# Attention scores: the second product of each head on half the rows, heads issued in pairs

## The chip, the cores and the metric

The kernel runs on one core of one Trainium2 chip. The metric is the device time of one execution in microseconds (us); where several runs are compared, their median. One core has TensorE (PE, matrix products; the loading of its stationary operand is listed apart as PEld), VectorE (DVE), ScalarE (ACT), GpSimd (POOL) and the queue that issues transfers (SP).

## What is computed

A two-layer trunk: in each layer a feed-forward sublayer, a mixer and a second feed-forward sublayer, for 512 latent tokens and 128 context tokens (640 columns, five tiles of 128). Both mixers hold an attention of 8 query heads of width 64 on 2 key heads; beside it runs a recurrent branch. The change touches the attention scores alone. The reference has

```
s = jnp.einsum('bqhgd,bkhd->bhgqk', q, k).astype(F32) * (q.shape[-1] ** -0.5)
if mask is not None: s = jnp.where(mask, s, NEG_INF)
...
p = jax.nn.softmax(s, axis=-1)
return jnp.einsum('bhgqk,bkhd->bqhgd', p.astype(v.dtype), v)
```

In the first mixer a latent tile sees its neighbour tiles (a band of +-128) and the 128 context keys, with a sink; in the second it sees all 512 latent keys and the 128 context keys. The context tile sees itself.

## The kernel before

Every product works on numbers split into a high part (rounded to the matmul format) and a low part (the remainder). Most products are three matmuls (`mm3`, high-high, high-low, low-high). The scores have a cheaper form, since a head has only 64 rows and TensorE takes 128: `q_stack` puts the high half of a head's query on 64 rows of a tile and its low half on the other 64. For heads 0 and 2 of a group of four the high half lies on rows 0 to 63, for heads 1 and 3 on rows 64 to 127. `att_keys` writes the keys' high part on both halves of the rows of `kk[:, 0]`, and their low part on both halves of `kk[:, 1]`. In `att_probs` the helper `scores` (L684) then needs two matmuls of 128 rows for a run of key tiles: stacked query times high keys, plus stacked query times low keys, added up in one PSUM bank.

`attention` goes through 10 steps: two key heads g, for each the five query tiles j. For a step `att_probs` takes the four heads in turn: it asks for a bank (`bank`, L112: PSUM tags a2 and b, two buffers each, used by other stages too), issues the scores, adds the mask on DVE, takes the row maximum on DVE, and has ACT compute the exponentials into SBUF. After heads 1 and 3 it yields. Then `att_out` transposes the probabilities on PE (tile pT, tag b), splits them on ACT and DVE and multiplies by the values (pv). In the first mixer a tile sees three or four key tiles, in one or two runs of neighbouring tiles; heads 0 to 2 have one bank each (a2 or b), head 3 one of three tiles and one of a single tile. In the second mixer a tile sees five key tiles, and every head has two parts, three tiles (384 columns, tag a2) and two tiles (256 columns, tag b). The fifth query tile has one key tile; all four heads then share one bank.

`weave` runs the attention's generator side by side with those of the projections (tiles pj and pn), one step of each in turn, so that one step of a projection (24 matmuls) follows each pair of heads in the text. The order on each engine is laid down before the run by the framework's planner, which starts from the order of the text and takes a later instruction where an earlier one isn't ready by its own reckoning (its operands, or a free bank). Each engine then works through its list in that order.

`mm` (L136) issues every matmul, so all of them have that line: they are told apart by tiles. The score matmuls are `s<-att`.

Of the kernel before, what the change touches and what calls it, by code (L numbers as in the profile page):

```python
# [17 lines left out]
P = 128  # L18
# [31 lines left out]
class Net:  # L50
# [628 lines left out]
    def att_probs(self, q, ks, tiles, masks, nsink, room, out):  # L679


        nc = self.nc
        mx, nm, su = self.sm(8, "mx"), self.sm(4, "nm"), self.sm(12, "su")

        def scores(o, hd, t0, t1):
            for n, k in enumerate(ks):
                self.mm(o, q[:, hd], k[:, t0 * P:t1 * P], n == 0, n == 1)

        def minus(c):
            if nsink is None:  # L690
                self.ts(nm[:, c], mx[:, c], -1.0, ALU.mult)
            else:
                self.stt(nm[:, c], mx[:, c], -1.0, nsink[:, c], ALU.mult, ALU.min)

        two = []
        if len(tiles) == 1:
            p = self.bank("a2", "s1")
            for hd in range(4):
                scores(p[:, hd * P:(hd + 1) * P], hd, tiles[0], tiles[0] + 1)
            nc.vector.tensor_reduce(out=mx[:, 0:4], in_=p.rearrange("p (a b) -> p a b", a=4), op=ALU.max, axis=AX.X)  # L700
            minus(slice(0, 4))
            for hd in range(4):
                r = room[hd][0][:, 0:P]
                self.act(r, p[:, hd * P:(hd + 1) * P], AF.Exp, bias=nm[:, hd:hd + 1], accum_out=su[:, hd:hd + 1])
                out.append([r])
            yield
        else:
            for hd in range(4):
                pos, parts, at = 0, [], []
                for r in room[hd]:  # L710
                    ts = tiles[pos:pos + r.shape[-1] // P]
                    pos += len(ts)
                    if not ts:
                        break
                    n = len(parts)
                    p = self.bank(("a2", "b")[n if len(room[hd]) > 1 else hd % 2], "s1")
                    o = 0
                    while o < len(ts):
                        e = o + 1
                        while e < len(ts) and ts[e] == ts[e - 1] + 1:  # L720
                            e += 1
                        scores(p[:, o * P:e * P], hd, ts[o], ts[e - 1] + 1)
                        o = e
                    p = p[:, :len(ts) * P]
                    if masks and n == 0:
                        v = p.rearrange("p (a b) -> p a b", b=P)[:, masks[0]]
                        self.tt(v, v, masks[1], ALU.add)
                    nc.vector.tensor_reduce(out=mx[:, 4 * n + hd:4 * n + hd + 1], in_=p, op=ALU.max, axis=AX.X)
                    parts.append((p, r[:, :len(ts) * P]))
                    at += [r[:, i * P:(i + 1) * P] for i in range(len(ts))]  # L730
                c = slice(hd, hd + 1)
                if len(parts) > 1:
                    self.tt(mx[:, c], mx[:, c], mx[:, 4 + hd:5 + hd], ALU.max)
                minus(c)
                for n, (p, r) in enumerate(parts):
                    self.act(r, p, AF.Exp, bias=nm[:, c], accum_out=su[:, 4 * n + hd:4 * n + hd + 1])
                if len(parts) > 1:
                    two.append(hd)
                out.append(at)
                if hd % 2 == 1:  # L740
                    yield
        if two:
            a, b = two[0], two[-1] + 1
            self.tt(su[:, a:b], su[:, a:b], su[:, 4 + a:4 + b], ALU.add)
        if nsink is not None:
            self.tt(su[:, 8:12], nm, nsink, ALU.subtract)
            self.act(su[:, 8:12], su[:, 8:12], AF.Exp)
            self.tt(su[:, 0:4], su[:, 0:4], su[:, 8:12], ALU.add)
        nc.vector.reciprocal(out=su[:, 4:8], in_=su[:, 0:4])
        for hd in range(4):  # L750
            n = len(tiles)
            for r in room[hd]:
                w = min(n, r.shape[-1] // P)
                n -= w
                if w:
                    self.ts(r[:, :w * P], r[:, :w * P], su[:, 4 + hd:5 + hd], ALU.mult)
# [810 lines left out]
```

## Time and profile before

| | |
|---|---|
| median of 3 runs | 2791.62 us (2791.42 to 2794.95) |
| profiled execution, whole | 2794.22 us |
| its span | 2792.4 us |
| PE busy | 2691.6 us, 96% |
| PEld busy | 2583.1 us, 93% |
| DVE, ACT, POOL busy | 1781.6, 947.6, 250.5 us |
| score matmuls | 260, in two stretches: 595 to 760 us and 1900 to 2110 us |

The profiled execution lies 2.6 us above the median, inside what the three runs show; 1.8 us of it lie outside the span. Matmul durations overlap, since a matmul's recorded end is modelled: what one matmul costs is read from the distance between the starts of matmuls that follow each other, not from its duration.

### The profile page before, as it was taken

What the parts mean: (1) busy time and instruction counts of PE and PEld (TensorE: products, weight loads), DVE (VectorE), ACT (ScalarE), POOL (GpSimd) and SP (SyncE); (2) the same over time, 40 slices, a digit from 0 to 9 for tenths busy, and PEclk for the clock granted to TensorE, in tenths of its full rate; (3) what the DMA queues carried; (4) which work ended last, traced back from release to release, by engine and by line L of the source; (5) the groups of instructions that cost most, each with busy time, mean ns of one, the idle gap of its engine ahead of it and who ended that gap; (6) DMA issues with size and microseconds to landing.
All of it is one profiled execution on the core that took longest, in us unless ns stands there. A gap on an engine that the chain in (4) does not pass through costs nothing.

```text
span 2792.4 us, 46713 instructions
## 1 busy us (share of the span) xinstructions
PE 2691.6 (96%) x19121; PEld 2583.1 (93%) x19121; DVE 1781.6 (64%) x3498; ACT 947.6 (34%) x1946; POOL 250.5 (9%) x293
## 2 busy tenths in 40 slices
PE   7999999999999999999999999999999899999998
PEld 4999999898888999999999999987888789999997
DVE  4967864676767976533896773375677688333335
ACT  3321221455554421311522122154555444112112
POOL 1000000410013000000400000051100031000003
PEclk9999999999999999999999999998999999999999
DMA  7553543221122544422264452121011225213210
GB/s 244 174 151 115 166 121 85 71 73 48 39 74 79 171 133 124 133 64 68 69 186 125 123 170 77 53 85 50 24 46 59 70 78 145 74 54 99 69 46 38
DMA packets 307186, 270.52 MB, mean 97 GB/s; under 512 B 13834, under 2 KB 257308, under 8 KB 306972
## 3 DMA queue, kind: packets, MB, share of 16 engines
q1 hardware_dynamic: 306612, 267.39, 32.2%
q8 instruction: 150, 2.46, 0.4%
q14 instruction: 64, 0.52, 0.1%
q10 hardware_dynamic: 360, 0.14, 0.0%
HBM read 258.31 MB, written 9.18 MB: 96 GB/s over the span
## 4 chain that ended last, share of the span: by engine, by line
PE 77%; DVE 11%; DMA 4%; ACT 4%; issue 2%; POOL 1%; DVEq 0%; ACTq 0%; SPq 0%; POOLq 0%
PE ps L136 36%; PE po L136 23%; PE pj L136 6%; PE pn L136 3%; DMA rawa<-in_ada_w 2%; DVE acc L133 2%; DVE w L126 2%; PE pv L136 1%; DMA raw<-in_ffn_w 1%; PE pT L139 1%; PE s L136 1%; DVE x L126 1%; DVE h L126 1%; DVE x L133 1%; DVE sum L126 1%
## 5 line engine op out<-in xcount | busy, mean ns | idle before, releaser
L136 PE MATMUL ps<-h,w 128*128 128x256 f32 (+1 forms) x7584 | 1123.5, 309 | 6.0 <-DVE h L126 3.2
L136 PEld LDWEIGHTS ps<-h,w 128*128 128x128 f32 x7584 | 1116.3, 190 | 8.6 <-DVE h L126 4.2
L136 PE MATMUL po<-g,wv 128*128 128x256 f32 (+1 forms) x4224 | 634.1, 310 | 8.2 <-DVE x L133 5.4
L136 PEld LDWEIGHTS po<-g,wv 128*128 128x128 f32 x4224 | 623.0, 189 | 15.7 <-DVE x L133 6.2
L133 DVE SCALAR_TENSOR_TENSOR x<-po,mod,x 128x128 f32<-128x128 f32 (+1 forms) x576 | 235.8, 435 | 280.5 <-PE po L136 278.2
L126 DVE TENSOR_TENSOR w<-raw,w 128x1024 fp32r<-128x1024 f32 x208 | 254.4, 1228 | 124.4 <-ACT w L123 123.6
L133 DVE SCALAR_TENSOR_TENSOR acc<-rawa,sc,acc 128x512 f32<-128x512 f32 x448 | 319.6, 757 | 11.7 <-DMA rawa<-in_ada_w 11.6
L123 ACT ACTIVATE wv<-raw 128x1024 fp32r<-128x1024 f32 x120 | 124.4, 1056 | 578.0 <-PE po L136 456.7
L123 ACT ACTIVATE w<-raw 128x1024 fp32r<-128x1024 f32 x208 | 218.6, 1056 | 160.5 <-issue 81.3
L485 POOL TENSOR_TENSOR ssq<-ssq,sq 128x384 f32<-128x384 f32 (+1 forms) x84 | 84.8, 1010 | 1726.4 <-ACT sq L123 1725.8
L123 ACT ACTIVATE g<-gt 128x384 fp32r<-128x384 f32 (+1 forms) x176 | 82.1, 466 | 403.8 <-DVE gt L126 403.7
L126 DVE TENSOR_TENSOR wv<-raw,wv 128x1024 fp32r<-128x1024 f32 x120 | 147.0, 1230 | 104.6 <-ACT wv L123 104.5
L126 DVE TENSOR_TENSOR gt<-sl,ps 128x384 f32<-128x384 f32 (+1 forms) x176 | 85.2, 484 | 181.5 <-PE ps L136 176.9
L136 PE MATMUL pj<-h,w 128*128 128x384 f32 (+1 forms) x864 | 150.6, 317 | 0.6 <-ACT mi L123 0.6
L123 ACT ACTIVATE sl<-ps 128x384 f32<-128x384 f32 (+1 forms) x176 | 76.0, 433 | 200.2 <-PE ps L136 199.9
L136 PE MATMUL ps<-h,wv 128*128 128x256 f32 (+1 forms) x864 | 139.4, 312 | 3.1 <-ACT h L123 1.3
L136 PE MATMUL pn<-w,h 128*128 128x256 f32 x960 | 139.5, 288 | 1.3 <-ACT mi L123 0.9
L136 PEld LDWEIGHTS pj<-h,w 128*128 128x128 f32 x864 | 132.5, 193 | 3.5 <-issue 1.2
L136 PEld LDWEIGHTS ps<-h,wv 128*128 128x128 f32 x864 | 128.4, 189 | 6.3 <-DVE h L126 3.0
L136 PEld LDWEIGHTS pn<-w,h 128*128 128x128 f32 x960 | 124.2, 190 | 4.2 <-ACT mi L123 1.1
L136 PE MATMUL pj<-h,wv 128*128 128x256 f32 (+1 forms) x672 | 114.1, 317 | 3.9 <-DVE t L126 1.8
L136 PEld LDWEIGHTS pj<-h,wv 128*128 128x128 f32 x672 | 100.7, 192 | 7.3 <-issue 2.1
(327 smaller groups left out, 2516.8 us busy)
## 6 DMA issues: line engine op xcount, KB each, us to landing
raw<-in_ffn_w SPq DMA_DIRECT2D x264, 512.0 KB
rawa<-in_ada_w SPq DMA_DIRECT2D x144, 512.0 KB
raw<-in_w_in_odd SPq DMA_DIRECT2D x18, 512.0 KB
raw<-in_w_in_even SPq DMA_DIRECT2D x14, 512.0 KB
raw<-in_w_in_even SPq DMA_DIRECT2D x16, 256.0 KB
raw<-in_w_out_even SPq DMA_DIRECT2D x8, 512.0 KB
raw<-in_w_in_odd SPq DMA_DIRECT2D x16, 256.0 KB
raw<-in_w_out_odd SPq DMA_DIRECT2D x8, 512.0 KB
```

Of the source, the lines that this page charges most:

```text
L123: return self.nc.scalar.activation(out=out, in_=in_, func=func, **k)
L126: return self.nc.vector.tensor_tensor(out=out, in0=in0, in1=in1, op=op)
L133: return self.nc.vector.scalar_tensor_tensor(out=out, in0=in0, scalar=s, in1=in1, op0=op0, op1=op1)
L136: return self.nc.tensor.matmul(out=out, lhsT=lhsT, rhs=rhs, start=start, stop=stop)
L139: self.nc.tensor.transpose(out, in_, self.ident[:in_.shape[0], :in_.shape[0]])
L485: nc.gpsimd.tensor_tensor(out=sums[1], in0=sums[1], in1=sq, op=ALU.add)
```

## The change

For a run of key tiles the first product stays as it is. The second product is issued apart (`rest`) and takes only the 64 rows on which the head's high query half lies: high query times low keys. The product of the two low halves is left out. The weights and the moving operand of this matmul are cut to rows 0 to 63 for heads 0 and 2, and to rows 64 to 127 for heads 1 and 3. The heads of a pair (0 and 1, 2 and 3) get their banks together, and their matmuls are issued for each run as: first product of one, first product of the other, second product of one, second product of the other. Masks, maxima and exponentials follow after both heads' scores. The step with one key tile keeps its two products on 128 rows.

```
         def scores(o, hd, t0, t1):
-            for n, k in enumerate(ks):
-                self.mm(o, q[:, hd], k[:, t0 * P:t1 * P], n == 0, n == 1)
+            self.mm(o, q[:, hd], ks[0][:, t0 * P:t1 * P], True, False)
+
+        def rest(o, hd, t0, t1):
+            r = slice(64 * (hd % 2), 64 * (hd % 2) + 64)
+            self.mm(o, q[r, hd], ks[1][r, t0 * P:t1 * P], False, True)
...
         if len(tiles) == 1:
             p = self.bank("a2", "s1")
             for hd in range(4):
-                scores(p[:, hd * P:(hd + 1) * P], hd, tiles[0], tiles[0] + 1)
+                c = slice(hd * P, (hd + 1) * P)
+                scores(p[:, c], hd, tiles[0], tiles[0] + 1)
+                self.mm(p[:, c], q[:, hd], ks[1][:, tiles[0] * P:tiles[0] * P + P], False, True)
...
+            banks = {}
             for hd in range(4):
+                if hd % 2 == 0:
+                    lists = []
+                    for h2 in (hd, hd + 1):
+                        pos, lst = 0, []
+                        for n, r in enumerate(room[h2]):
+                            ts = tiles[pos:pos + r.shape[-1] // P]
+                            pos += len(ts)
+                            if not ts:
+                                break
+                            p = banks[h2, n] = self.bank(("a2", "b")[n if len(room[h2]) > 1 else h2 % 2], "s1")
+                            o = 0
+                            while o < len(ts):
+                                e = o + 1
+                                while e < len(ts) and ts[e] == ts[e - 1] + 1:
+                                    e += 1
+                                lst.append((p[:, o * P:e * P], h2, ts[o], ts[e - 1] + 1))
+                                o = e
+                        lists.append(lst)
+                    for n in range(max(map(len, lists))):
+                        for f in (scores, rest):
+                            for lst in lists:
+                                if n < len(lst):
+                                    f(*lst[n])
...
-                    p = self.bank(("a2", "b")[n if len(room[hd]) > 1 else hd % 2], "s1")
-                    o = 0
-                    while o < len(ts):
-                        e = o + 1
-                        while e < len(ts) and ts[e] == ts[e - 1] + 1:
-                            e += 1
-                        scores(p[:, o * P:e * P], hd, ts[o], ts[e - 1] + 1)
-                        o = e
-                    p = p[:, :len(ts) * P]
+                    p = banks[hd, n][:, :len(ts) * P]
```

## Rows read from the trace of the kernel before

**Rows 1.** The page: busy time by engine, and the chain that ended last.

```profile
PE 2691.6 (96%) x19121; PEld 2583.1 (93%) x19121; DVE 1781.6 (64%) x3498; ACT 947.6 (34%) x1946; POOL 250.5 (9%) x293
...
PE 77%; DVE 11%; DMA 4%; ACT 4%; issue 2%; POOL 1%; DVEq 0%; ACTq 0%; SPq 0%; POOLq 0%
```

**Rows 2.** Busy time in the two stretches: us, each engine's (instructions), clock, DMA.

```profile
595.00:760.00 165.00, 159.72 (x1079) 145.64 (x1079) 116.79 (x310) 91.64 (x240) 9.64 (x17) 0.99 0.17 47
1900.00:2110.00 210.00, 198.50 (x1377) 172.87 (x1376) 146.70 (x386) 118.52 (x315) 16.81 (x18) 0.96 0.13 37
```

**Rows 3.** Tile s by form: weight rows*columns, moving rows x columns, count | busy, mean.

```profile
L136 PE MATMUL s<-att 128*128 128x384 f32 x100 | 29.2, 374 | 4.6 <-ACT pq L123 4.0 <-ACT E L123 0.4
L136 PE MATMUL s<-att 128*128 128x256 f32 x80 | 17.5, 303 | 0.1
L136 PE MATMUL s<-att 128*128 128x128 f32 x68 | 10.5, 257 | 0.0
...
L136 PE MATMUL s<-att 128*128 128x512 f32 x12 | 4.2, 402 | 0.3 <-ACT bm L123 0.3
```

**Rows 4.** Timeline of PE, first mixer: start us, us, engine, line, tiles, form, count.

```profile
598.18 3.04 PE L136 MATMUL pn<-w,h 128*128 128x256 f32 x24
601.06 1.03 PE L136 MATMUL s<-att 128*128 128x256 f32 x8
601.92 3.09 PE L136 MATMUL pn<-w,h 128*128 128x256 f32 x24
...
606.21 4.43 PE L136 MATMUL pj<-h,w 128*128 128x384 f32 x24
610.48 0.38 PE L139 MATMUL pT<-ident,E 128*128 128x128 f32 x2
610.70 0.27 PE L139 MATMUL pT<-ident,bm 128*128 128x128 f32 x1
```

**Rows 5.** Timeline of PE around matmuls with 64 weight rows (nmu, ab).

```profile
751.16 1.21 PE L136 MATMUL pj<-h,w 128*128 128x256 f32 x8
752.30 0.79 PE L136 MATMUL ab<-ma,identr 64*128 64x384 f32 x4
...
754.55 0.85 PE L136 MATMUL pn<-w,h 128*128 128x256 f32 x5
755.33 0.50 PE L136 MATMUL nmu<-ma,identr 64*128 64x256 f32 x2
755.76 1.22 PE L136 MATMUL pn<-w,h 128*128 128x256 f32 x8
756.91 0.50 PE L136 MATMUL nmu<-ma,identr 64*128 64x256 f32 x2
```

**Rows 6.** Timeline of PE: a matmul with 64 weight columns among full ones.

```profile
632.32 0.40 PE L136 MATMUL pv<-pr,vals 128*64 128x512 f32 x1
632.55 0.62 PE L136 MATMUL s<-att 128*128 128x512 f32 x2
633.02 0.63 PE L136 MATMUL pv<-pr,vals 128*64 128x512 f32 x2
```

**Rows 7.** Timeline of PE: matmuls on 32 weight columns each, at the kernel's start.

```profile
16.51 0.62 PE L136 MATMUL ada<-rawa,scz 128*32 128x512 f32 x2 [0.23 <-DMA rawa<-in_ada_w]
```

**Rows 8.** Groups by form, 16.4 to 17.7 us: count | busy us, mean ns | idle.

```profile
L136 PE MATMUL ada<-rawa,scz 128*32 128x512 f32 x4 | 1.1, 604 | 0.2 <-DMA rawa<-in_ada_w 0.2
```

**Rows 9.** Timeline of PE, first mixer: two heads of one step.

```profile
623.80 0.62 PE L136 MATMUL s<-att 128*128 128x512 f32 x2
...
628.15 0.40 PE L136 MATMUL s<-att 128*128 128x512 f32 x1
```

**Rows 10.** Timeline of PE, second mixer: scores among a projection's matmuls.

```profile
2044.35 0.60 PE L136 MATMUL s<-att 128*128 128x384 f32 x2
...
2045.32 0.51 PE L136 MATMUL s<-att 128*128 128x256 f32 x2
...
2047.28 0.61 PE L136 MATMUL s<-att 128*128 128x384 f32 x2
```

## The prediction

> **What bounds the kernel now.** I read the page first. TensorE is busy for 2691.6 of 2792.4 us, 96%, and the chain that ended last runs on it for 77% of the span; VectorE has 64%, ScalarE 34% [rows 1]. So a change of the attention is worth what it does to PE's own list of matmuls, as long as nothing else becomes late. The score matmuls lie in two stretches, and the table of busy time by stretch shows there what the page shows for the whole: PE busy for 159.7 of 165 us and 198.5 of 210, at a granted clock of 0.99 and 0.96, with VectorE and ScalarE at 56 to 71% [rows 2]. PE is idle for 5.3 and 11.5 us, 16.8 together. That is all the slack that the two stretches have, and it belongs to PE's waits for the softmax, not to the matmuls.
>
> Next I counted the score matmuls by form: 100 of 384 columns, 80 of 256, 68 of 128 and 12 of 512, 260 in all, every one with 128 weight rows [rows 3]. 32 of the 128-column ones belong to the step with one key tile, which stays as it is. Of the other 228 half are second products: 50 of 384 columns, 40 of 256, 18 of 128, 6 of 512, that is 114 `rest` matmuls. They are 0.6% of PE's 19121 matmuls, so the whole change is about tens of us at the most.
>
> Then the price of one. A matmul's recorded duration overlaps its neighbours', so the reader should look at starts. 24 matmuls of 256 columns take from 598.18 to 601.06 us, 0.120 us each; 24 of 384 columns from 606.21 to 610.48, 0.178 each; two of 128 columns 0.11 each [rows 4]. Two of 512 take from 632.55 to 633.02, 0.235 each [rows 6]. These distances follow the columns, so no weight load lies open between them.
>
> **What the change can save.** The number of matmuls and weight loads stays. A matmul with 64 rows streams as many columns as one with 128, so alone it saves nothing. What can be saved is the second product of a pair's second head, if it runs beside the first head's on the other half of the rows. The loops give 56 pairs of `rest` and two without a partner (the lone tile of head 3 at j = 2, once for each g): 24 pairs of 384 columns, 20 of 256, 8 of 128, 2 of 512, and 2 of 512 with 384. At the prices above: 24 x 0.178 + 20 x 0.120 + 8 x 0.11 + 2 x 0.235 + 2 x 0.178 = 8.4 us, if every pair overlaps in full. No row of before has two matmuls on different halves of the rows back to back. The nearest are matmuls on different strips of 32 columns: two of 512 columns start and end within 0.62 us, hardly more than one of them lasts (mean 0.604), so strips of columns do run side by side [rows 7, 8]. I take full overlap for adjacent partners; the bounds are nothing and 8.4 us.
>
> **What a change of rows costs.** The kernel already has matmuls of the very form that `rest` gets, 64 weight rows by 128 columns: nmu (rows 0 to 63) and ab (rows 64 to 127) of the recurrent branch. They are the rows that decide the case [rows 5]. Between two groups of them eight full matmuls of 256 columns take from 751.16 to 752.30, 1.14 us, where 8 x 0.120 = 0.96 was due; five take 0.78 for 0.60; eight take 1.15 for 0.96. And two nmu of 256 columns take from 755.33 to 755.76, 0.43 for 0.24. So every stretch between two changes of form carries 0.18 to 0.19 us that its matmuls don't explain, on both sides. One excursion to 64 rows and back costs 0.37 us, whether it holds two matmuls or four. By these rows PE doesn't stream across the change: the pipeline has to run empty, and then the weight load of the next matmul lies open. A cut of the columns has no such price: a matmul of 64 weight columns is followed by a full one after 0.23 us, the ordinary distance of 512 columns [rows 6].
>
> The Trainium skill has a rule that speaks against the change: TensorEngine Tiling (Array Packing), Key Properties, says that a change of the tiling mode, not merely of the tile, drains TensorE. The rows with 64 weight rows agree; those with 64 weight columns don't show it, so the rule taken alone would price the pv matmuls too, and the measurement decides. With the rule and without a figure for it the sum could not be made; with the rows it can.
>
> **The sum.** If all partners stay adjacent, there are 58 excursions: 58 x 0.37 = 21.5 us, less the 8.4 saved, is +13.1 us. That is the lower bound of PE's own time. If every `rest` stands alone, 114 x 0.37 = 42.2 us and nothing saved: the upper one.
>
> Which is it? PE's list is laid out beforehand, and an instruction that isn't ready gives way to the next that is. The scores of a head are ready when its PSUM bank is free. In the text `rest` of the first head now stands behind the first product of the second, but if the second head's bank isn't free at that moment, `rest` of the first is ready and goes alone. In the first mixer at j = 0 the eight score matmuls of a pair stand together [rows 4]; there the partners will stay adjacent (4 pairs for each g), and I expect the same for the second pair at j = 1 (2 more). At j = 2 the two heads' scores lie 4.35 us apart, since the second waits for a bank of tag b, which the transposes use too [rows 9]; I count j = 2, j = 3 and the first pair of j = 1 as broken: 6 of 12 pairs for each g. That makes 12 adjacent pairs, 24 lone halves and 2 single ones, 38 excursions. In the second mixer the scores stand one by one among projection matmuls, about 1 to 3 us apart, as banks come free [rows 10], so I count all 32 pairs as broken, 64 excursions. Sum: 102 x 0.37 = 37.7 us, less what the 12 adjacent pairs save (2 x (2 x (0.120 + 0.11) + 0.178 + 0.11) = 1.5 us), is +36.2 us of PE time.
>
> Not all of it reaches the end. Of PE's 16.8 us of idle time [rows 2] a part is waiting for the softmax of an earlier head; matmuls that take longer in between use it up. A delay ahead of the scores pushes the softmax back as well and uses up nothing. Bounds 0 and 16.8 us; I take half, 8.4 us, leaving +27.8 us.
>
> Edits that I cost at nothing: the instructions on VectorE and ScalarE are the same in number and form. Their start moves: the first head's maximum now waits for the second head's first product and for the excursion, some 0.18 + 0.37 us. VectorE has 30% of the stretch free to cover that; if it hadn't, 16 pairs of heads in each stretch would add 32 x 0.55 = 18 us, which is within the upper half of the range together with the cushion. The new wait is that of a second head's first product for its bank; on PE the first head's `rest` and the projection's matmuls queue behind it where the planner's reckoning was too early, and VectorE's maximum waits with them. Before, PE lost 4.6 us in front of 384-column scores in that way, 4.0 of them for ScalarE [rows 3]; doubled, that is 5 us more, and with good timing nothing or a little less. I take zero and keep 5 for the range.
>
> From the profiled execution (2794.2 us) the sum gives 2822 us; it lies 2.6 above the median, so against the runs' median of 2791.6 I predict 2819.4 us.
>
> **The rivals.** (1) The planner keeps the partners adjacent nearly everywhere. Then +13.1, less a share of the cushion of about 4: 2801 us. For it speaks the order of the text, and [rows 4]; against it [rows 9, 10]. (2) The change pays: the 64-row matmuls of two heads run side by side and the change of form costs nothing, as with 64 columns [rows 6]. Then -8.4: 2783 us, faster. The point from which this decides is the price of an excursion: below 8.4 / 58 = 0.145 us the change gains. Against it stand all four stretches of [rows 5], at 0.37. By the Trainium skill (TensorE: Matmul & The Clock Gate, Part 3, The mechanism) matmuls on different row groups start about 4 ns apart; by that alone this rival would be the result, and no row of before shows it for rows. (3) The excursions happen, but PE's idle time swallows them: with adjacent partners the 13.1 us would fit into the 16.8 idle, and the time would stay within 0.2%, at about 2793. It needs the waits to lie behind the excursions everywhere. (4) Everything is broken up, nothing is absorbed, and the new bank waits add 5: up to 42.2 + 2 or 3 on the median, 2836 us. The edit that changes nothing, because `rest` would still be taken as a 128-row matmul, I exclude: nmu and ab are cut by the same slices of rows and stand as 64*128 in the trace.
>
> **How the numbers follow.** Forecast 0.60; rival 1 0.19; rival 2 0.06; rival 3 0.05; rival 4 0.10. About 0.2%, 5.6 us, is what a measurement of this kernel can tell from no change. Faster 0.06 (rival 2), same 0.06 (rival 3 and a little of rival 1), slower 0.88. The range leaves out rivals 2 and 3 and the far end of rival 4: 2800 to 2836 us. Everything in it is slower than before.
>
> **What would show it.** In the profile after, tile s should have 146 matmuls of form 128*128 and 114 of 64*128; wherever a 64*128 group begins or ends, the starts should lie some 0.18 us further apart than columns explain, and PE's idle time of kind "issue" should grow in both stretches. PE's count stays at 19121. Lone groups should outnumber pairs, above all in the second mixer. Outside the two stretches nothing should move. I am wrong if adjacent partners cost more than 0.37 us together (no overlap), if lone excursions are rare, or if the two stretches don't lengthen although the excursions are there.

## The result and the profile after

The changed kernel takes 2823.22 us (median of 5 runs, 2816.15 to 2823.36) against 2791.62 of before; the ratio is 1.0099 with an interval of 1.0088 to 1.0109, so it is slower by 25 to 30 us. The two medians lie 31.6 us apart, a little more than this interval, since the five runs spread over 7 us. The profiled execution took 2823.36 us with a span of 2821.6, 29.2 us more than before. Forecast were 2819.4 and a range of 2800 to 2836.

The page of the changed kernel, busy times and chain, answers to [rows 1]:

```profile
PE 2728.3 (97%) x19121; PEld 2591.9 (92%) x19121; DVE 1784.8 (63%) x3498; ACT 947.5 (34%) x1946; POOL 252.0 (9%) x293
...
PE 81%; DVE 9%; DMA 4%; ACT 2%; issue 2%; POOL 1%; SPq 0%; ACTq 0%; DVEq 0%; POOLq 0%
```

The counts are those of before on every engine. PE's busy time has grown by 36.7 us and that of its weight loads by 8.8, no other by more than 3.2, and the chain runs on PE for 81% of the span instead of 77%. The score matmuls of the changed kernel by form answer to [rows 3]:

```profile
L136 PE MATMUL s<-att 64*128 64x384 f32 x50 | 21.9, 448 | 0.0
L136 PE MATMUL s<-att 128*128 128x384 f32 x50 | 18.7, 378 | 2.1 <-ACT pq L123 2.0
L136 PE MATMUL s<-att 64*128 64x256 f32 x40 | 13.3, 381 | 0.0
...
L136 PE MATMUL s<-att 64*128 64x128 f32 x18 | 4.2, 323 | 0.0
L136 PE MATMUL s<-att 64*128 64x512 f32 x6 | 3.0, 497 | 0.0
```

They are the 114 second products. A matmul with half the rows is recorded as longer than one with all (448 ns on average for 384 columns, 378 for the first products), because its start is recorded together with that of its own weight load, which lies open (two such rows are shown below, for the pn behind a `rest`).

Where did the time go? I divided both traces at the mixers. Each runs from the row sums of the sublayer before it to the row sums behind it: the first from 532 to 876 us, the second from 1856 to 2281. Busy time by stretch, kernel before (us, then PE, PEld, DVE, ACT, POOL with their instructions, granted clock, DMA):

```profile
532.00:876.00 344.00, 328.18 (x2179) 300.50 (x2178) 245.28 (x656) 180.69 (x490) 42.66 (x66) 0.98 0.24 64
1856.00:2281.00 425.00, 389.99 (x3628) 344.59 (x3628) 298.17 (x669) 210.24 (x534) 53.31 (x56) 0.96 0.20 59
```

The same two stages of the changed kernel:

```profile
532.00:887.00 355.00, 341.29 (x2180) 302.12 (x2178) 246.35 (x657) 179.91 (x489) 43.22 (x66) 0.97 0.23 62
1867.00:2309.00 442.00, 410.63 (x3628) 348.36 (x3628) 299.60 (x668) 210.09 (x534) 53.50 (x56) 0.96 0.19 56
```

The mixers are longer by 11 and 17 us, 28 of the 29.2. PE is busy for 13.1 and 20.6 us more, and idle for 2.1 and 3.6 less. DVE and ACT are busy for as long as before, to within 1.5 us, and the clock agrees to 0.01. So nearly all of it is PE's own time in the two mixers, and most of that lies among the scores: from the first to the last score matmul the mixers grew by 7.2 and 17.7 us (132.8 to 140.0, 176.4 to 194.1). Against the prediction, 3.9 us of the first mixer's 11 come behind its last scores, where no matmul changed its form. Six pj matmuls that now stand there make about 1 us of it; the rest stays open.

One stretch shows how. In the second mixer the planner laid out the same list in both kernels: scores of 384 columns, three pn, scores of 256, thirteen pn, and so on. Timeline of PE in the changed kernel (start us, us, engine, line, tiles, form, count):

```profile
2067.84 0.69 PE L136 MATMUL s<-att 128*128 128x384 f32 x2
2068.47 0.62 PE L136 MATMUL pn<-w,h 128*128 128x256 f32 x3
2068.93 0.59 PE L136 MATMUL s<-att 128*128 128x256 f32 x2
2069.44 1.81 PE L136 MATMUL pn<-w,h 128*128 128x256 f32 x13
...
2075.39 0.70 PE L136 MATMUL s<-att 128*128 128x384 f32 x2
```

Each s row holds one first product and one lone `rest` (the row prints the form of its first). From 2067.84 to 2075.39 are 7.55 us and five excursions; before, the same instructions took from 2044.35 [rows 10] to 2050.36 (below), 6.01 us. That is 0.31 us for an excursion on average. The fourth of the five shows the price with nothing else in the way, changed kernel, then kernel before:

```profile
2072.13 0.59 PE L136 MATMUL s<-att 128*128 128x256 f32 x2
2072.65 0.62 PE L136 MATMUL pn<-w,h 128*128 128x256 f32 x3
2073.11 0.70 PE L136 MATMUL s<-att 128*128 128x384 f32 x2
```

```profile
2047.85 0.40 PE L136 MATMUL s<-att 128*128 128x256 f32 x2
2048.09 0.52 PE L136 MATMUL pn<-w,h 128*128 128x256 f32 x3
2048.44 0.51 PE L136 MATMUL s<-att 128*128 128x384 f32 x2
```

The two scores take 0.52 us to the next pn and took 0.24 before; the three pn take 0.46 and took 0.35. That is 0.28 and 0.11, together 0.39. The price read from nmu and ab [rows 5] is there in full.

Why, then, only 0.31 on average? The kernel before paid something in the place of the first two excursions. Its weight loads and matmuls there, and the end of the stretch:

```profile
2044.78 0.51 PE L136 MATMUL pn<-w,h 128*128 128x256 f32 x3
...
2045.32 0.30 PEld L136 LDWEIGHTS s<-att 128*128 128x128 f32 x2 [0.23 <-ACT E L123]
...
2045.55 0.42 PEld L136 LDWEIGHTS pn<-w,h 128*128 128x128 f32 x3
2045.66 0.40 PE L136 MATMUL pn<-w,h 128*128 128x256 f32 x2
...
2050.36 0.62 PE L136 MATMUL s<-att 128*128 128x384 f32 x2
```

The weight load stood idle for 0.23 us ahead of the score's, waiting for ScalarE's exponentials, that is for its bank; three pn took 0.54 us for 0.36. In the changed kernel PE arrives later and the bank is free. So the first two excursions add only 0.12 and 0.27 us, the other three 0.36 to 0.40. And after the scores of 256 columns at 2045.32 the next weight load begins 0.11 us ahead of its matmul, hidden, while in the changed kernel both begin together:

```profile
2069.44 0.30 PEld L136 LDWEIGHTS pn<-w,h 128*128 128x128 f32 x2
2069.44 0.39 PE L136 MATMUL pn<-w,h 128*128 128x256 f32 x1
```

What the engines wait for before they touch tile s says the same, with one difference from the prediction. Changed kernel, then kernel before (releaser: total us, times):

```profile
  issue: 18.1, 81
```

```profile
  issue: 0.7, 2
```

"issue" is time in which nothing that the profile shows was waited for: 81 times in front of scores, 18.1 us. All of it stands on the weight loads (PEld). The prediction had asked for more idle time of this kind on PE itself; that did not come: recorded matmuls overlap across such a place, so it counts as busy, and PE's idle time shrank.

### The profile page after: what moved, and what is told of

Its sections match the earlier page's. It is cut to its first block, busy times and chain, and to the rows that moved or that the text cites. A ratio compares the mean times of both kernels' runs of the same rounds, so it can differ in the third digit from the quotient of the medians.

```text
span 2821.6 us, 46722 instructions
## 1 busy us (share of the span) xinstructions
PE 2728.3 (97%) x19121; PEld 2591.9 (92%) x19121; DVE 1784.8 (63%) x3498; ACT 947.5 (34%) x1946; POOL 252.0 (9%) x293
## 4 chain that ended last, share of the span: by engine, by line
PE 81%; DVE 9%; DMA 4%; ACT 2%; issue 2%; POOL 1%; SPq 0%; ACTq 0%; DVEq 0%; POOLq 0%
PE ps L136 37%; PE po L136 23%; PE pj L136 7%; PE pn L136 4%; DMA rawa<-in_ada_w 2%; DVE acc L133 2%; PE s L136 2%; PE pv L136 1%; DVE w L126 1%; DMA raw<-in_ffn_w 1%; PE pT L139 1%; PE num L136 1%; DVE x L133 1%; DVE x L126 1%; DVE sum L126 1%
```

## The experiments

My theory: each entry into matmuls of 64 rows and each return costs PE about 0.18 us, and partners overlap only where they are adjacent. Rivals: the pairwise issue costs the time, through PSUM banks and a later softmax, and the row cut is free; or 64 rows are just slower matmuls. Medians below stand beside the median of the kernel before on the same chip, which lies between 2791.6 and 2795.9.

**own_head: the row cut without pairs.**

```
 def scores(o, hd, t0, t1):
+    r = slice(64 * (hd % 2), 64 * (hd % 2) + 64) if len(tiles) > 1 else slice(0, P)
-    for n, k in enumerate(ks):
-        self.mm(o, q[:, hd], k[:, t0 * P:t1 * P], n == 0, n == 1)
+    self.mm(o, q[:, hd], ks[0][:, t0 * P:t1 * P], True, False)
+    self.mm(o, q[r, hd], ks[1][r, t0 * P:t1 * P], False, True)
```

> The second product is cut to 64 rows as in the change, but the heads are issued one after the other as before: no partner ever stands beside it, banks are asked for as before. Theory (each entry into 64-row matmuls and each return costs about 0.18 us): 114 excursions at 0.37 us are 42 us of PE time; the change kept about three quarters of its own 36, so 32 to 38 us over before, 2823 to 2830. Rival (the pairwise issue and its bank waits cost the time, the row cut is free): no more than 3 us from before.

2822.85 us against 2794.39, ratio 1.0105 (1.009 to 1.012). 28.5 us, somewhat below my 32 to 38, and no pair in sight: the row cut alone costs what the change costs. In the trace all 114 `rest` stand alone, 50 in the first mixer and 64 in the second. 28.5 / 114 is 0.25 us of each excursion that reaches the end.

**pair_full: pairs without the row cut.**

```
 def rest(o, hd, t0, t1):
-    r = slice(64 * (hd % 2), 64 * (hd % 2) + 64)
+    r = slice(0, P)
```

> Heads in pairs, in the order of the change, but the second product on all 128 rows as before. Theory (price of the change of rows): within 3 us of before, 2789 to 2795. Rival (pairwise issue): most of the 31 us of the change, 2810 or more. A third, that 128-row products in pairs lose a few us to bank waits: 2795 to 2800.

2797.56 against 2794.39, ratio 1.0018 (1.0009 to 1.0028): 3 to 8 us. The pairwise issue costs little, but I had put it at nothing; of the three outcomes written down, the third came (a few us). The two profiled executions show no place for it (spans 2792.7 and 2792.4 us), so where these few us lie stays open.

**rows96: fewer rows, but more than half.**

```
-    r = slice(64 * (hd % 2), 64 * (hd % 2) + 64)
+    r = slice(0, 96) if hd % 2 == 0 else slice(0, P)
```

> Pairs as in the change, but the second product takes rows 0 to 95 for heads 0 and 2 and all 128 for heads 1 and 3 (the sums hold half of the low-low product for those heads, or all of it). 57 matmuls then have 96 rows. Theory, if the price belongs to the switch to half the rows: as with 128 rows in pairs, about 2792. If any count of rows below 128 has the price: 57 excursions at 0.37 us, 21 us, of which some 16 are kept, 2808. Rival (pairwise issue): as the 128-row pairs, whatever that is.

2796.56 against 2794.39, ratio 1.0008 (0.9999 to 1.0017). The heads come in pairs here too, and the whole comes to less than 5 us: 56 matmuls of 96 rows cost nothing that can be told from the pairwise issue. Groups by form and PE's timeline of this kernel, in the stretch with the same list as above:

```profile
L136 PE MATMUL s<-att 96*128 96x384 f32 x24 | 8.5, 356 | 0.0
L136 PE MATMUL s<-att 96*128 96x256 f32 x20 | 5.7, 282 | 0.0
```

```profile
2045.52 0.59 PE L136 MATMUL s<-att 128*128 128x384 f32 x2
...
2049.61 0.52 PE L136 MATMUL s<-att 128*128 128x384 f32 x2
2049.97 1.71 PE L136 MATMUL pn<-w,h 128*128 128x256 f32 x13
...
2051.55 0.63 PE L136 MATMUL s<-att 128*128 128x384 f32 x2
```

6.03 us from 2045.52 to 2051.55, as before (6.01), though three of the five scores in it have their second product on 96 rows; the one at 2049.61, in a place where the kernel before had no wait, is followed after 0.36 us, the ordinary 2 x 0.178. So the price doesn't belong to fewer rows as such. The Trainium skill (TensorEngine Tiling (Array Packing), Tiling Modes) lists row tilings of 64 and 32 rows and none of 96; read with the drain that its Key Properties give to a change of mode, 96 rows, which have no mode of their own there, would be free, and the trace agrees.

**full_nmu: the price taken away elsewhere.** The kernel before, with nmu and ab on 128 rows:

```
-    self.mm(nmu[:, :b - a], self.identr[0:64, r:r + 1].to_broadcast([64, P]), ma[q][0:64, a:b], ...)
+    self.mm(nmu[:, :b - a], self.identr[:, r:r + 1].to_broadcast([P, P]), ma[q][:, a:b], ...)
...
-    self.mm(ab[:, :b - a], self.identr[64:128, 64 + r:64 + r + 1].to_broadcast([64, P]), ma[q][64:128, a:b], ...)
+    self.mm(ab[:, :b - a], self.identr[:, 64 + r:64 + r + 1].to_broadcast([P, P]), ma[q][:, a:b], ...)
```

> The kernel before, its scores untouched; the 64-row matmuls nmu and ab of the recurrent branch take all 128 rows (the rows added have zero weights). Theory: about 30 excursions vanish, 30 x 0.37 = 11 us of PE time, of which three quarters or more reach the end: 2780 to 2785. Rival (row cut is free, those stretches wait for something else): 2791, unchanged.

2786.22 against 2794.39, ratio 0.9972 (0.9961 to 0.9983). More rows in the same matmuls, and the kernel is 8.2 us faster. The 29 excursions of before are gone. PE's timeline of this kernel, at the list of [rows 5]:

```profile
751.84 0.75 PE L136 MATMUL pn<-w,h 128*128 128x256 f32 x5
752.43 0.39 PE L136 MATMUL nmu<-ma,identr 128*128 128x256 f32 x2
752.66 1.11 PE L136 MATMUL pn<-w,h 128*128 128x256 f32 x8
753.61 0.39 PE L136 MATMUL nmu<-ma,identr 128*128 128x256 f32 x2
```

Five pn now take 0.59 us (0.78 in [rows 5]), two nmu 0.23 (0.43), eight pn 0.95 (1.15). This is the cleanest proof of the price: the list is the same, only the rows differ, and about 0.39 us go with each excursion. Of 29 of them 8.2 us reached the end, 0.28 each.

**adjacent and adj_full: the order pinned.** Each of a pair's matmuls is laid out behind the one before it (`scores` and `rest` now return their matmul), once with the row cut and once with r = slice(0, P):

```
...
-for n in range(max(map(len, lists))):
-    for f in (scores, rest):
-        for lst in lists:
-            if n < len(lst):
-                f(*lst[n])
+last = None
+for n in range(max(map(len, lists))):
+    group = [lst[n] for lst in lists if n < len(lst)]
+    for f in (scores, rest):
+        for one in group:
+            with ExitStack() as order:
+                if last is not None:
+                    order.enter_context(self.tc.issue_after(last.ins))
+                last = f(*one)
```

> The change, with its order pinned: a pair's four matmuls are laid out first product, first product, rest, rest, each behind the one before it, so that nearly all partners stand side by side (about 60 to 65 excursions instead of 103). Theory: 63 x 0.37 = 23 us, less some 7.5 for partners that run together, 16 us of PE time, of which three quarters are kept, and up to 5 for pairwise issue: 2804 to 2811. Rival (what costs is that PE's list waits for the second head's bank): pinning makes it worse than the change, 2825 or more.

> The pinned order with the second product on all 128 rows: what the order and its bank waits cost with no change of rows. Theory: 0 to 5 us over before, about as the pairs that were not pinned (2797). Rival (waits for banks): 10 us or more over before.

adjacent: 2830.91 against 2795.89, ratio 1.0125 (1.011 to 1.014). adj_full: 2820.51, ratio 1.0088 (1.007 to 1.0106). Both of my numbers failed, and the rival that I had written beside them, waits for banks, came true. Pinning works as meant: 51 of 56 pairs stand together in the trace, with 63 excursions. But with no change of rows at all the pinned order costs 24.6 us, five times what I allowed. PE's waits in the second mixer of adj_full (total us, times, longest):

```profile
PE lv L136 <- ACT xarena L123: 13.5, 7, 2.9
PE s L136 <- ACT pq L123: 9.3, 8, 2.7
```

and in the kernel before:

```profile
PE lv L136 <- ACT xarena L123: 4.3, 6, 1.0
PE s L136 <- ACT pq L123: 4.0, 5, 1.6
```

Busy time in that stage of adj_full:

```profile
1859.00:2304.00 445.00, 395.96 (x3628) 351.43 (x3628) 297.41 (x670) 210.02 (x535) 55.02 (x57) 0.93 0.19 56
```

Scores wait 5.3 us more for banks that ScalarE holds. The matmuls lv of the recurrent branch wait 9.2 us more: four groups of them, each waiting 2.1 to 2.4 us, now stand one behind the other from 2208 us on, where the kernel before has other matmuls between them. So a part of the 24.6 us comes from this one layout of the list; the other 10 are not placed. Over this control the row cut costs 10.4 us, and all four runs with it lie above all four without. That agrees with the theory: 63 excursions at 0.25 us kept (own_head) to 0.27 (28.0 us over the 103 of the changed kernel) are 16 to 17, less what 51 overlapped pairs save.

**same_half: the same pinned order, no different halves.** adjacent with r = slice(0, 64) for both heads.

> As the pinned one, but both heads' second products take rows 0 to 63, so partners are on the same rows (heads 1 and 3 get low query times low keys instead of high times low). Same excursions, no two of them on different halves. Theory (partners on different halves run at the same time, starts some 4 ns apart): 7 us more PE time than the pinned one, 5 to 7 us slower than it. Rival (adjacent 64-row matmuls gain nothing from different halves): the same time as the pinned one.

2837.66 against 2830.91 of adjacent: 6.8 us for the overlap of 51 pairs, as expected; all four runs lie above all four of adjacent. One group of seven recorded score matmuls (384 and 256 columns, two heads) in adjacent and the same seven in same_half, from the timeline of each:

```profile
1962.13 1.46 PE L136 MATMUL s<-att 128*128 128x384 f32 x7
```

```profile
1970.37 1.74 PE L136 MATMUL s<-att 128*128 128x384 f32 x7
```

0.28 us less, where one matmul of 384 and one of 256 columns are 0.178 + 0.120. This also settles the last rival: a second matmul on 64 rows of the same half takes the ordinary time of its columns, so 64 rows are not slower in themselves. And a pair of the changed kernel itself, at 601.7 to 601.8 us:

```profile
601.57 0.33 PE L136 MATMUL s<-att 64*128 64x128 f32 x2
```

Two matmuls within 0.33 us, when one of this form lasts 0.323 on average: partners on different halves do run at the same time. The Trainium skill (TensorE: Matmul & The Clock Gate, Part 3, The mechanism) says about 4 ns between such starts; the records of all 11 pairs here and all 51 of adjacent show 3 to 4.

**once: fewer excursions.** adjacent, with both parts of a head in one group in the second mixer:

```
...
+groups = [[lst[n] for lst in lists if n < len(lst)] for n in range(steps)]
+if len(room[hd]) > 1:
+    groups = [sum(groups, [])]
```

> Pinned, and in the second mixer both parts of both heads first get their four first products, then the four rests: one excursion for a pair instead of two, some 16 to 20 there and about 30 in the first mixer, 48 in all. Theory: 48 x 0.37 = 17.8 less 8, about 10 us of PE time, kept 7, plus up to 5 for the order: 2800 to 2806, 4 us faster than the pinned one. Rival (waits for four banks at once on PE): slower than the pinned one.

2829.41, ratio 1.0118 (1.0101 to 1.0135), against 1.0125 of adjacent. 47 excursions instead of 63, but 1.5 us instead of 4, and the runs of the two overlap: this tells nothing apart.

**no_rest: the second product left out.** The kernel before with only the first product for runs in steps of several key tiles.

```
-for n, k in enumerate(ks):
-    self.mm(o, q[:, hd], k[:, t0 * P:t1 * P], n == 0, n == 1)
+one = len(tiles) > 1
+self.mm(o, q[:, hd], ks[0][:, t0 * P:t1 * P], True, one)
+if not one:
+    self.mm(o, q[:, hd], ks[1][:, t0 * P:t1 * P], False, True)
```

> The kernel before without the second product of the 114 runs (the low part of the keys is left out of those scores): no added form, no pairs. It takes away 50 x 0.178 + 40 x 0.120 + 18 x 0.11 + 6 x 0.235 = 17.1 us of PE time. Theory (PE's own work in these stretches reaches the end at about three quarters): 12 to 15 us less than before, ratio 0.995. Rival (the stretches are held by the softmax and PE's work is a filler): less than 4 us.

2783.12 against 2795.25, ratio 0.9956 (0.994 to 0.9972). 12.1 of 17.1 us, 71%; the interval allows 7.8 to 16.8 us. With own_head's 28.5 of 42, what PE is given or spared in these stretches reaches the end at about seven tenths, in both directions.

**full_rows: also the 2-row matmuls on 128.** full_nmu, and the matmul qrb on 128 rows with zeroed ones added:

```
...
-self.mm(pb[:, :b - a], bsel, rr[0:2])
+self.mm(pb[:, :b - a], bsel, rr)
```

> As the kernel with nmu and ab on 128 rows, and also the 2-row matmuls (qrb) of the second mixer's norms on 128 rows, with zero rows added: 20 matmuls that entered and left a cut of the rows 10 times. Theory: 10 x 0.37 = 3.7 us less PE time, some of it under waits for ScalarE, so 1 to 3 us better than the 0.9972 of that kernel: 0.996 to 0.997. Rival (a cut to 2 rows isn't such a switch, or its price is hidden by the wait before it): 0.997, no change, or worse by the zeroing.

2784.01 against 2795.25, ratio 0.9956 (0.9941 to 0.9971). It beats both kernels. That it is better than full_nmu (0.9972) is likely by the medians but not told apart: the intervals overlap.

## Why the prediction was right, and where it wasn't

**The price of an excursion** was the term that decided, read from rows of another branch before the change existed: 0.37 us. The list of full_nmu gives 0.39, the undisturbed excursions in the stretch of the changed kernel 0.36 to 0.40. Right.

**The count**: forecast were 38 excursions in the first mixer and 64 in the second; the trace has 40 and 63. 11 pairs stayed together (forecast 12), ten of them in the first mixer. The reading of [rows 4, 9, 10] held: where scores wait singly for banks, the second head's first product isn't ready and the first head's `rest` goes alone.

**The saving** by overlap, 8.4 us for 56 pairs, was the estimate with the least ground, from column strips. same_half puts it at 6.8 us for 51: right. One price in it was off: the 0.11 us for 128 columns was read from transposes (pT) and doesn't follow the columns; at the price of the columns it is 0.06, which takes 0.4 from the 8.4. The change reaps the saving for 11 pairs only.

**The sum on PE and the cushion.** Forecast were +36.2 us of PE time less 8.4 of idle time used up, +27.8. The stages show +33.7 busy and -5.7 idle, +28.0. That the difference came out so closely is partly luck: both terms were about 2.5 us too large, and a share of one half was chosen without a row to show it. The clean stretch shows what I had pictured wrongly. I looked for the cushion in PE's idle time, but a part of it stands in no idle column: a score that waits 0.2 us for its bank overlaps the recorded end of the matmul before it, so it counts as busy, and an excursion that comes ahead of it replaces that wait.

**What I put at nothing.** The pairwise issue: pair_full has 3 to 8 us. This is a term that was mis-sized, by a few us at the most, since rows96 with the same pairs shows less than 5; with pair_full's figure in the sum the forecast would have been 2822 to 2827. The new wait of the second head's first product for its bank cost little in the change, since the planner let the first head's `rest` pass.

**The rivals.** Rival 1, partners adjacent at 2801 us, failed in its own sum. It had the excursions and the overlap right (10.4 us over its control), but took the order as free, and the order that keeps partners together here costs 24.6 us, waits of the recurrent branch included. So 2801 was not to be had by this pinning; another order that keeps the pairs was not tried. Rival 2 was half true: partners overlap fully, yet the change of form has its price, far above the 0.145 us up to which the change would gain. Rival 3 failed: the idle time in the two mixers shrank by 5.7 us only. Rival 4 was the right direction for own_head, whose 114 lone excursions cost 28.5 us and not 42: the same seven tenths.

**Left open**: where the few us of pair_full lie, what makes up the 10 us of the pinned order that aren't placed, and whether once gains what its count of excursions says.

## What to carry to other kernels

Before cutting the rows of a matmul, look at its neighbours in the engine's list: between full matmuls a lone one on half the rows cost 0.37 to 0.39 us of PE time here, more than twice its own 0.12 to 0.18 us of streaming. By these prices the cut can pay only where several such matmuls stand together and their partners lie on other rows, which no run here reached; and what keeps them together may cost more than it saves. In the other direction it is worth searching a tuned kernel for small matmuls with 64 rows or fewer and filling their rows with zero weights: here that was the only change that gained without leaving a product out.

## What the runs showed of the hardware that I had not expected

A matmul on 96 rows goes in and out among full ones at no price (6.03 us for a stretch of 6.01), and so does one on 64 weight columns [rows 6]; one on 64 rows pays about 0.2 us on either side. Two matmuls on different halves start 3 to 4 ns apart and take the time of one. And with the pinned order the clock was lower where PE waited more: in the second mixer of adj_full the granted clock averaged 0.93, against 0.96 before, while PE stood idle for 49 of 445 us instead of 35 of 425. An average below 1 means that some of it ran at 1.2 GHz instead of 2.4.
